# Output projection of a hybrid encoder layer: the attention half of the first 1024 columns by seven block products instead of eight

## The chip, the cores and the metric

One core of one Trainium2 chip runs the whole kernel. The metric is the device time of one execution in microseconds (us). The engines are named as the profile names them: PE (matrix products), PEld (weight loads of PE), ACT, DVE, POOL and SP (which only issues transfers). ACT and POOL issue transfers too.

## The reference, cut to what matters

One encoder layer is computed for 768 rows (a prompt of 512 and a sample of 256) of width 2048:

```python
h = rmsnorm(x, ln_mix_g); z = h @ w_in              # fourier group | q | k | v
of = fourier_mix(zf, w_fourier)                     # 768 x 1024
oa = window_attention(q, k, v, attn_sink)           # 768 x 1024
mixed = concatenate([rmsnorm(of, g_f), rmsnorm(oa, g_a)])
x = x + mixed @ w_out                               # 2048 x 2048; the second half of its rows meets oa
h = rmsnorm(x, ln_mlp_g); u = relu(h @ w_up); x = x + (u * u) @ w_down
return rmsnorm(x, ln_final_g)
```

The change is in the second half of `mixed @ w_out`: `oa` (768 x 1024) times rows 1024 to 2047 of `w_out`.

## The kernel before, in words

All arithmetic is float32 in effect: each operand of a product is split into a high part `h` (rounded) and a low part `l` (the rest), and a product is three matmuls, `h*wh + h*wl + l*wh`. ACT makes the high part by a copy (or a copy with a gain), DVE makes the low part by a subtraction.

Rows come in six tiles `m` of 128, columns of `w_out` in four groups `n` of 512, the 1024 channels of `oa` in eight blocks `k` of 128. In the stage of attention the Fourier half of `w_out` is multiplied in and put to memory as `y1_d[m][n]`; the attention blocks go to memory as `oa_d[m]` (transfers named `oad`) and come back as `oah`/`oal` (`load_oa`). The stage after it, called here the projection stage, does the attention half. For each `n` it takes three pairs of row tiles, `(mp, mp + 3)`; one pair is 48 matmuls of 512 columns into the two banks of `pm` (`proj_slot`). Then `x1_rows` adds: `sums` (DVE: `y1 + x`, which POOL has added up, plus `pm` times the row factor `r2`), `squares` (ACT), and `factors`: eight transposes on PE into `pt`, and `x1_factors` on DVE and ACT, which for `n < 2` makes the seven left factors `xf` of the next stage (`up_product`, which itself already works with seven products).

Weights come by `out_load(i)` (SP, 512 KB) and `out_split(i)`, where `i` numbers pieces of two `k` blocks by 512 columns; 16 to 19 are the attention half of `n = 0`, 20 to 23 of `n = 1`. `out_split` with a gain is, for each of the two `k` blocks, one ACT copy with the gain as scale and one DVE instruction.

The order of work is written by hand: `at(t, fn)` and `later(dt, fn)` put a step into a list by time, where one unit is six matmuls of 512 columns (two blocks `k` of one row tile, or one `k` of a pair), and `run_events(t)` is called between matmuls and records the steps that are due. Under `manual_schedule` PE, ACT, DVE, POOL and SP each run their instructions in the order in which they are recorded. So the list sets the order on every engine, and an instruction that waits holds up those recorded behind it on its engine. The DMA transfers of SP and ACT use eight semaphores (`DMAHW0` to `DMAHW7`) in turn, in the order in which they are recorded, and a transfer waits for the one that had its semaphore before it, which is the one eight places ahead.

## Time and profile before

| | |
|---|---|
| median of 3 runs | 2563.78 us (2563.24 to 2564.96) |
| the profiled execution, its own time | 2563.83 us |
| its span, first to last instruction | 2562.0 us |
| granted PE clock, mean | 0.999 |
| busy share of the span, PE / PEld / DVE / ACT / POOL | 100% / 91% / 71% / 44% / 11% |
| projection stage, first to last matmul start | 564.0 to 705.6 us |
| matmuls of 512 columns in it, besides 11 groups of 8 transposes | 576 |

Times in the profile are microseconds from the start of the span. Matmuls are pipelined: one of 512 columns is shown with some 389 ns, but the next starts after some 227 ns, so a short wait of PE hides in the overlap, and the count of matmuls in a stretch tells more than PE's busy share. `SPq` and `ACTq` are the issues of transfers.

### The profile page before, as it was taken

What the parts mean: (1) busy time and instruction counts of PE and PEld (TensorE: products, weight loads), DVE (VectorE), ACT (ScalarE), POOL (GpSimd) and SP (SyncE); (2) the same over time, 40 slices, a digit from 0 to 9 for tenths busy, and PEclk for the clock granted to TensorE, in tenths of its full rate; (3) what the DMA queues carried; (4) which work ended last, traced back from release to release, by engine and by line L of the source; (5) the groups of instructions that cost most, each with busy time, mean ns of one, the idle gap of its engine ahead of it and who ended that gap; (6) DMA issues with size and microseconds to landing.
All of it is one profiled execution on the core that took longest, in us unless ns stands there. A gap on an engine that the chain in (4) does not pass through costs nothing.

```text
span 2562.0 us, 34695 instructions
## 1 busy us (share of the span) xinstructions
PE 2552.0 (100%) x13415; PEld 2336.7 (91%) x13415; DVE 1810.6 (71%) x2144; ACT 1127.7 (44%) x1630; POOL 272.6 (11%) x387
## 2 busy tenths in 40 slices
PE   9999999999999999999999999999999999999998
PEld 9999998888899999999999999988888888888887
DVE  7877767678466556556777777667766756777687
ACT  7454557674233333334445454433333333333335
POOL 0023333223201010100000000200000000000000
PEclk9999999999999999999999999999999999999999
DMA  7686386465745444466666666775543662554364
GB/s 294 229 285 214 115 245 193 138 179 187 236 163 186 159 165 163 165 207 225 231 230 214 217 215 216 277 279 176 176 146 124 221 222 89 176 183 157 101 211 153
DMA packets 261029, 496.99 MB, mean 194 GB/s; under 512 B 21147, under 2 KB 145569, under 8 KB 260737
## 3 DMA queue, kind: packets, MB, share of 16 engines
q1 hardware_dynamic: 193600, 332.00, 40.7%
q10 hardware_dynamic: 51360, 101.43, 10.5%
q0 software_dynamic: 15904, 61.36, 7.1%
q8 instruction: 105, 1.72, 0.3%
q14 instruction: 60, 0.48, 0.1%
HBM read 373.19 MB, written 121.51 MB: 193 GB/s over the span
## 4 chain that ended last, share of the span: by engine, by line
PE 98%; DMA 1%; DVE 0%; ACT 0%; issue 0%; POOL 0%; SPq 0%; ACTq 0%; DVEq 0%; POOLq 0%
PE pu L1390 36%; PE pd L1825 35%; PE pm L1243 10%; PE p L287 7%; PE pz L1001 3%; PE pv L543 1%; PE o L1122 1%; PE s L1045 1%; PE t L1100 1%; PE pa L796 0%; PE ptx L138 0%; PE pe L815 0%; DMA ofd<-of 0%; DMA raw<-in_w_out 0%; DMA xr<-in_x_t 0%
## 5 line engine op out<-in xcount | busy, mean ns | idle before, releaser
L1390 PE MATMUL pu<-xf,wh 128*128 128x384 f32 x3072 | 780.2, 334 | 0.0
L1390 PEld LDWEIGHTS pu<-xf,wh 128*128 128x128 f32 x3072 | 554.1, 188 | 1.5 <-ACT o L1408 1.3
L1825 PE MATMUL pd<-wh,sh 128*128 128x512 f32 x1332 | 517.7, 389 | 0.0
L1825 PE MATMUL pd<-wl,sh 128*128 128x512 f32 x1332 | 517.7, 389 | 0.0
L1825 PE MATMUL pd<-wh,sl 128*128 128x512 f32 x1332 | 517.5, 389 | 0.0
L1390 PE MATMUL pu<-xf,wl 128*128 128x384 f32 x1536 | 513.1, 334 | 0.0
L1802 ACT ACTIVATE wh<-rd 128x1024 fp32r<-128x1024 f32 x200 | 202.4, 1054 | 522.3 <-PE pd L1825 424.4
L1812 DVE TENSOR_TENSOR wl<-rd,wh 128x1024 fp32r<-128x1024 f32 x200 | 236.1, 1221 | 226.2 <-ACT wh L1802 225.5
L1370 ACT ACTIVATE wh<-ur 128x1024 fp32r<-128x1024 f32 x160 | 170.1, 1063 | 382.6 <-PE pu L1390 226.7
L1825 PEld LDWEIGHTS pd<-wl,sh 128*128 128x128 f32 x1332 | 250.0, 188 | 51.9
L1825 PEld LDWEIGHTS pd<-wh,sh 128*128 128x128 f32 x1332 | 250.0, 188 | 51.9
L1825 PEld LDWEIGHTS pd<-wh,sl 128*128 128x128 f32 x1332 | 249.9, 188 | 51.8 <-DVE sl L1813 0.3
L1390 PEld LDWEIGHTS pu<-xf,wl 128*128 128x128 f32 x1536 | 288.3, 188 | 0.0
L1376 DVE TENSOR_TENSOR wl<-ur,wh 128x1024 fp32r<-128x1024 f32 x160 | 195.5, 1222 | 76.1 <-ACT wh L1370 76.1
L1411 DVE TENSOR_TENSOR o<-pu,o 128x768 f32<-128x768 f32 x160 | 152.9, 956 | 122.4 <-PE pu L1390 114.9
L287 PE MATMUL p<-xs,wh 128*128 128x384 f32 x672 | 170.6, 334 | 0.0
L1795 DVE TENSOR_TENSOR rd<-rd 128x1024 f32<-128x1024 f32 x112 | 131.7, 1217 | 0.0
L1390 PE MATMUL pu<-xs,wh 128*128 128x384 f32 x512 | 129.8, 334 | 0.0
L1370 ACT ACTIVATE wh<-sx 128x1024 fp32r<-128x1024 f32 x64 | 67.9, 1062 | 130.5 <-PE pu L1390 104.3
L287 PEld LDWEIGHTS p<-xs,wh 128*128 128x128 f32 x672 | 121.4, 188 | 0.1
L287 PE MATMUL p<-xs,wl 128*128 128x384 f32 x336 | 112.2, 334 | 0.0
L1813 DVE TENSOR_TENSOR sl<-sr,sh 128x768 fp32r<-128x768 f32 x111 | 105.6, 951 | 0.0
(309 smaller groups left out, 3774.9 us busy)
## 6 DMA issues: line engine op xcount, KB each, us to landing
rd<-in_w_down SPq DMA_DIRECT2D x176, 512.0 KB, 5.2
ur<-in_w_up SPq DMA_DIRECT2D x128, 512.0 KB, 3.8
sr<-sd SPq DMA_DIRECT2D x95, 384.0 KB, 5.4
pd<-o ACTq DMA_DIRECT2D x60, 384.0 KB, 2.3
o<-pd POOLq DMA_DIRECT2D x60, 384.0 KB, 6.2
sd<-sm ACTq DMA_DIRECT2D x60, 384.0 KB, 2.8
raw<-in_w_in SPq DMA_DIRECT2D x40, 512.0 KB, 5.1
raw<-in_w_out SPq DMA_DIRECT2D x32, 512.0 KB, 4.5
```

The source lines that it names most:

```text
L287: nc.tensor.matmul(ps7[own, g, r][:, :HALF], l[:, i, r * P : (r + 1) * P], x[:, o, 4 * e + i, :], start=(opens and e == 0 and i == 0 and q ...
L1001: nc.tensor.matmul(ps[c][s][:, :HALF], w[:, i, cs], whole[j // 2][s][o][:, 4 * (j % 2) + i, :], start=first and n == 0, stop=stop and n == 2,)
L1243: nc.tensor.matmul(ps, l(k), w[:, k % 2, :], start=(k == 0 and n == 0), stop=(k == 7 and n == 2))
L1370: nc.scalar.activation(wh[:], raw[:], AF.Copy)
L1376: nc.vector.tensor_tensor(out=wl[:], in0=raw[:], in1=f32(wh[:]), op=ALU.subtract)
L1390: nc.tensor.matmul(ps[:, t, :HALF], w[:, i, t * P : (t + 1) * P], xb[:, o, i, :], start=(s == first_of[bank] and i == 0 and n == 0), stop= ...
L1411: nc.vector.tensor_tensor(out=o, in0=src, in1=o, op=ALU.add)
L1795: add = lambda x, y, op: nc.vector.tensor_tensor(out=x[:], in0=x[:], in1=y[:], op=op)
L1802: nc.scalar.activation(wh[:], t[:], AF.Copy)
L1812: nc.vector.tensor_tensor(out=wl[:], in0=t[:], in1=f32(wh[:]), op=ALU.subtract)
L1813: nc.vector.tensor_tensor(out=sl[:], in0=sr[:], in1=f32(sh[:]), op=ALU.subtract)
L1825: nc.tensor.matmul(o, l[:, q, ts], w[:, ns], start=(j == j0 and (q, t) == (0, 0)), stop=(j == j1 and (q, t) == (1, 2)),)
```

## The change: what it does

For `n = 0` and `n = 1` the row tiles are taken as two blocks (tiles 0 to 2 and 3 to 5), the channels as two halves, and the 1024 columns as two halves, and the eight block products become seven, with sums of weight blocks (`ws1`, `ws2`, `s3`, `s4`) and of row blocks (`rows_sum`). The products run in the order of `steps`: a11, a12, s2, s1, s3, s4, a22. Each is 3 row tiles `p` by 4 `k` blocks by 3 matmuls. What a product gives is added by DVE into the rows that it belongs to (`add_rows`).

- Matmuls of 512 columns in this part: 7 x 36 = 252, before 288. `n = 2` and `n = 3` stay as they were, 288.
- Weights: pieces 16 to 19 (a11, a12) are split as before, but the gain is put in first, in place (`out_scale`, two ACT copies), and then comes one ACT copy and one DVE subtraction over the whole piece. The same is so for pieces 24 to 31. Blocks a21 and a22 (pieces 20 to 23) are loaded by `block_load` and scaled; a12 is loaded a second time. Ten further pieces are made by `block_high` and `block_low`, eight pieces' worth of sums by `block_sum`.
- Rows: for each `p`, four blocks of 128 x 512 are loaded a second time from `oa_d` (`rows_load`), four subtractions make the sums, and four splits the parts (`rows_parts`).
- Transposes and `x1_factors` of the first six pairs no longer stand between the products but beside `n = 2` and `n = 3`, at 42.8, 45.4, 48.0, 57.2, 64.3 and 72.3; the finished rows wait in `yq` and `op` tiles. The tile `xf` is opened only behind the products.

The diff, cut to its core:

```diff
     def out_split(i, more=True):
         half, n, j = out_seq[i]
-        k0 = half * 8 + 2 * j
-        out_w[half, n].append(wsplit(raws.pop(i), (lambda r: gcat[:, k0 + r : k0 + r + 1]) if half else None))
+        raw = raws.pop(i)
+        if half:
+            out_scale(i, raw)
+        out_w[half, n].append(wsplit(raw))
+        if 16 <= i < 18:
+            first_raw.append(raw)
...
+        def block_load(name):
+            for i, w in enumerate(ws[name]):
+                n, k0 = int(name[1]) - 1, 8 + 4 * (int(name[2]) - 1) + 2 * i
+                nc.sync.dma_start(w[:], w_out[:, k0 : k0 + 2, n * 512 : (n + 1) * 512])
...
+        def rows_sum(p, i):
+            b = rows[p]
+            x, y = ((1, 0), (2, 1), (2, 0), (3, 2))[i]
+            sub(b[i], b[x], b[y])
...
+        def rows_parts(f, p):
+            raw = rows[p][{3: 0, 4: 1, 5: 2, 6: 3}[f]]
+            nc.scalar.activation(th[f][p][:], raw, AF.Copy)
+            later(u_tl, lambda: sub(tl[f][p][:], raw, f32(th[f][p][:])))
...
+        block_load("a21")
+        rows_load(0)
+        block_load("a22")
+        for half in range(3):
+            turn_load(half, 0, None)
+        rows_load(1)
+        load_oa(5, lambda dt, fn: later(u_oa + dt, fn), spare)
+        rows_load(2)
+        block_scale("a21")
+        block_scale("a22")
+        rows_first(0)
+        at(0.2, lambda: rows_second(0))
+        at(0.3, lambda: row_factors(0, 5))
+        at(1.1, lambda: rows_first(1))
+        at(2.0, lambda: block_sum("s1", "a21", "a22", ALU.add))
+        at(4.0, lambda: block_sum("s2", "s1", "a11", ALU.subtract))
+        at(5.2, lambda: rows_second(1))
+        at(7.0, lambda: rows_first(2))
...
+        at(14.8, lambda: row_factors(5, 6))
+        for name, t in (("s2", 6.2), ("s1", 12.2), ("s3", 20), ("s4", 25), ("a22", 30.6)):
+            for i in range(2):
+                at(t + 1.1 * i, lambda name=name, i=i: block_high(name, i))
...
+        for q, (name, f, bank) in enumerate(steps):
+            for p in range(3):
...
+                for k in range(4):
+                    wh, wl = parts7[name][k // 2]
+                    for n, (o, w) in enumerate(((0, wh), (0, wl), (1, wh))):
+                        nc.tensor.matmul(
...
+        for half, t in enumerate((42.8, 45.4, 48.0, 57.2, 64.3, 72.3)):
+            at(t, lambda half=half: factors_of(half // 3, half % 3, yps.pop(half)))
```

The next three pieces show where the instructions stand. The first is the end of ACT's work for the attention stage: `raw` are the weight pieces 16 to 19, `os` and `xc` the last results that go to memory as `oad` and `y1`. Before:

```order
L72 ACTIVATE wh_6474<-raw_5853,gall_258 128x512 x2
L72 ACTIVATE wh_6488<-raw_5905,gall_258 128x512 x2
L1130 COPY os_6504<-o_6499 64x512
L72 ACTIVATE wh_6510<-raw_5931,gall_258 128x512 x2
L1275 ACTIVATE xc_6516<-pm_6447,r1_262 128x512
L1138 DMA oad5_97<-os_6504 64x4x128
L72 ACTIVATE wh_6519<-raw_5951,gall_258 128x512 x2
L1276 DMA y1_5_3_121<-xc_6516 128x512
```

The same place of the change:

```order
L171 ACTIVATE raw_5853<-raw_5853,gall_258 128x512 x2
L69 ACTIVATE wh_6476<-raw_5853 128x1024
L171 ACTIVATE raw_5905<-raw_5905,gall_258 128x512 x2
L69 ACTIVATE wh_6488<-raw_5905 128x1024
L1142 COPY os_6500<-o_6495 64x512
L171 ACTIVATE raw_5931<-raw_5931,gall_258 128x512 x2
L69 ACTIVATE wh_6508<-raw_5931 128x1024
L1287 ACTIVATE xc_6512<-pm_6447,r1_262 128x512
L1150 DMA oad5_97<-os_6500 64x4x128
L171 ACTIVATE raw_5951<-raw_5951,gall_258 128x512 x2
L69 ACTIVATE wh_6517<-raw_5951 128x1024
L1288 DMA y1_5_3_121<-xc_6512 128x512
```

Each weight piece has one more ACT instruction, of 1024 elements, and two whole pieces stand ahead of the copy `os`, whose result ACT's `oad5` transfer sends.

The second piece is SP's queue at the border of the two stages, with the semaphores for which each transfer waits. Before:

```order
L79 DMA raw_6480<-in_w_out 128x2x512 [waits DMAHW2_49,DVE_49]
L79 DMA raw_6494<-in_w_out 128x2x512 [waits DMAHW3_49,DVE_49]
L1547 DMA cx_6634<-y1_0_0_98 128x512 [waits DMAHW6_49,DMAHW5_49,DMAHW7_49,DMAHW1_49,DVE_49]
L1550 DMA xr_6636<-in_x_prompt 128x512 [waits PE_49]
L1547 DMA cx_6634<-y1_3_0_110 128x512 [waits DMAHW0_49]
```

The change, from the two transfers of block a22 to the third of the rows of `p = 1`:

```order
L1627 DMA wa22_6654<-in_w_out 128x2x512 [waits DMAHW2_49]
L1627 DMA wa22_6655<-in_w_out 128x2x512 [waits DMAHW3_49,Pool_49]
L1556 DMA yp_6662<-y1_0_0_98 128x512 [waits DMAHW4_49,DVE_49]
L1560 DMA xr_6678<-in_x_prompt 128x512 [waits DMAHW5_49]
L1556 DMA yp_6664<-y1_1_0_102 128x512 [waits DMAHW6_49,PE_49]
L1560 DMA xr_6682<-in_x_prompt 128x512 [waits DMAHW7_49]
L1556 DMA yp_6665<-y1_2_0_106 128x512 [waits DMAHW0_49]
L1560 DMA xr_6686<-in_x_prompt 128x512 [waits DMAHW1_49]
L1649 DMA b_6650<-oad1_93 128x4x128 [waits DMAHW2_49]
L1649 DMA b_6651<-oad4_96 128x4x128 [waits DMAHW3_49]
L1649 DMA b_6652<-oad4_96 128x4x128 [waits DMAHW4_49]
```

Eight places ahead of `wa22_6654` in the recorded order stands ACT's transfer `oad5<-os`, and eight ahead of `wa22_6655` ACT's `y1_5_3<-xc`, the last two of the first piece (SP's six between them, `wa21` twice and `b` four times, are recorded behind these two). `b_6651` has the semaphore of `wa22_6655`.

The third piece is DVE. Behind the low parts of the four weight pieces and the four row sums of `p = 0` stands this, up to the first weight piece of product s2 (`wl_6808`), which PE reads from its 74th matmul of the stage on:

```order
L1608 TENSOR_TENSOR b_6652<-b_6652,b_6650 128x512
L1635 TENSOR_TENSOR ws1_6630<-wa21_6648,wa22_6654 128x1024
L1635 TENSOR_TENSOR ws1_6631<-wa21_6649,wa22_6655 128x1024
L1581 SCALAR_TENSOR_TENSOR yp_6662<-pm_6713,r2_263,yp_6662 128x512
L1635 TENSOR_TENSOR ws2_6628<-ws1_6630,raw_5853 128x1024
L1635 TENSOR_TENSOR ws2_6629<-ws1_6631,raw_5905 128x1024
L1581 SCALAR_TENSOR_TENSOR yp_6664<-pm_6735,r2_263,yp_6664 128x512
L1608 TENSOR_TENSOR lb_6641<-b_6646,hb_6638 128x512
L1608 TENSOR_TENSOR b_6653<-b_6653,b_6652 128x512
L1608 TENSOR_TENSOR lb_6642<-b_6652,hb_6639 128x512
```

and behind these, in this order, one more `add_rows`, three row sums of `p = 2`, and `wl_6808`; ahead of the first row stand the sums `b_6650` and `b_6651`. In the kernel before DVE had here, behind the low parts of the weights:

```order
L1575 SCALAR_TENSOR_TENSOR cx_6634<-pm_6653,r2_263,cx_6634 128x512 x2
L70 TENSOR_TENSOR oal5_6642<-cx_6634,oah5_6641 128x512 x2
L98 TENSOR_SCALAR r2_263<-pr_6744 128x1 x2
L1306 TENSOR_TENSOR cx_6777<-ptx_6751,gall_258 128x512 x2
L1313 TENSOR_TENSOR cx_6777<-cx_6777 128x512
L1313 TENSOR_TENSOR cx_6777<-cx_6777 128x256 x2
```

The sums of rows and weights thus stand in one queue with the adding up of the products, and the factors of `xf` have left this place.

More of the change, by code (lines that the diff above doesn't have):

```diff
@@ new lines, in turn_loads, with row_factors @@
+        def turn_loads(half):
+            yp = op.tile([P, 2, 512], F32, tag=f"of{'lh'[half % 2]}5", name="yp")
+            yps[half] = [yp[:, s, :] for s in range(2)]
+            for s in range(2):
+                turn_load(half, s, max(8 * half - 6 + u_xr - clock[0], 2.3))
+        def row_factors(m0, m1):
+            pr = pq.tile([P, 2, 512], F32, tag="pt", name="pr", bufs=1)
+            for m in range(m0, m1):
+                nc.tensor.matmul(pr[:, 0, m : m + 1], oa[m][2][:], ones[:, 0:1], start=True, stop=True)
+            rsqrt_of(r2[:, m0:m1], pr[:, 0, m0:m1], NH * HD, m1 - m0)
@@ new lines, in hybrid_encoder @@
+        ws = {"a11": first_raw, "s1": ws1, "s2": ws2, "a21": wa21, "a22": duo("wa22")}
+        rows.append(four(2))
+        spare = [sp.tile([P, 4, P], F32, tag=f"ob{i}", name="ob")[:] for i in range(2)]
+        ws["s3"], ws["s4"], ws["a12"] = ws["a21"], ws["s2"], ws["s1"]
+        def block_load(name):
+            for i, w in enumerate(ws[name]):
+                n, k0 = int(name[1]) - 1, 8 + 4 * (int(name[2]) - 1) + 2 * i
+                nc.sync.dma_start(w[:], w_out[:, k0 : k0 + 2, n * 512 : (n + 1) * 512])
```

211 lines of the change are left out of this document (143 added, 68 removed).

## The prediction

> **What bounds the kernel now.** I read the page first, its busy shares and the chain that ended last.
>
> ```profile
> PE 2552.0 (100%) x13415; PEld 2336.7 (91%) x13415; DVE 1810.6 (71%) x2144; ACT 1127.7 (44%) x1630; POOL 272.6 (11%) x387
> ...
> PE 98%; DMA 1%; DVE 0%; ACT 0%; issue 0%; POOL 0%; SPq 0%; ACTq 0%; DVEq 0%; POOLq 0%
> ```
>
> The chain is PE for 98% of the span. Next the waits of PE, all of them:
>
> ```profile
> PE pw L566 <- DVE ssx L133: 1.0, 1, 1.0
> PE pv L543 <- ACT xs L72: 0.6, 1, 0.6
> PE pm L1245 <- DVE ofl L1227: 0.3, 1, 0.3
> PE pm L1243 <- ACT ofh L1226: 0.2, 1, 0.2
> ```
>
> None lies in the projection stage. A matmul taken away is therefore worth its full interval, and a wait put in costs its full length. The interval is read from the chain in order of time:
>
> ```profile
> 563.48 6.14 PE pm L1243 x27
> 569.62 0.34 PE pr L1564 x4
> ...
> 582.28 10.94 PE pm L1243 x48
> ```
>
> 48 matmuls of 512 columns take 10.94 us, 0.228 each. By the view of the tile `pm` the stage starts at 564.0:
>
> ```profile
> L1243 PE MATMUL pm<-wh,oah x192: 389/389/486, 564.0 to 705.1; 128*128 128x512 f32 x192
> ```
>
> DVE's mean of 71% says little about this stage, so I read it in stretches:
>
> ```profile
> 588.00:612.00 24.00, 24.00 (x118) 20.14 (x117) 21.40 (x32) 12.58 (x21) 4.00 (x4) 1.00 0.59 194
> ...
> 636.00:660.00 24.00, 24.00 (x115) 20.06 (x115) 14.70 (x20) 6.14 (x12) 5.58 (x4) 1.00 0.65 201
> 660.00:684.00 24.00, 24.00 (x115) 20.05 (x115) 12.22 (x17) 8.08 (x17) 5.16 (x4) 1.00 0.76 249
> 684.00:705.80 21.80, 21.80 (x106) 18.20 (x106) 6.44 (x8) 4.84 (x10) 5.87 (x5) 1.00 0.68 220
> ```
>
> The fourth busy time is DVE's: 21.4 of 24 us in one stretch of the first half, 33 of 70 in the last three. The change gives DVE more work early in the stage, where it must be done before a product can start.
>
> **What is removed.** 288 - 252 = 36 matmuls: 36 x 0.228 = 8.2 us. The eighty-eight transposes and six single columns for the row factors stay in number and only move, so they cost nothing more on PE unless they wait.
>
> **The first product that needs new operands.** Products a11 and a12 use the old rows and pieces 16 to 19; s2 follows behind 72 matmuls, at 564.0 + 72 x 0.228 + 0.34 (the row factors) = 580.7. Its second matmul needs `wl_6808`. I follow the three queues to it. ACT first, from its timeline at the end of the attention stage:
>
> ```profile
> 558.86 0.69 ACT L1104 ACTIVATE th<-t,r 128x512 fp32r<-128x512 f32 x1
> 558.88 0.58 ACTq L1276 DMA_DIRECT2D y<-xc  x1
> 559.51 2.57 ACT L72 ACTIVATE wh<-raw,gall 128x512 fp32r<-128x512 f32 x4
> 563.51 0.58 ACT L1130 COPY os<-o 64x512 f32<-64x512 f32 x1 [1.44 <-PE o L1122]
> ...
> 564.85 0.61 ACTq L1138 DMA_DIRECT2D oad<-os  x1
> ...
> 566.08 0.33 ACTq L1276 DMA_DIRECT2D y<-xc  x1
> ```
>
> ```profile
> L1802 ACT ACTIVATE wh<-rd 128x1024 fp32r<-128x1024 f32 x200 | 202.4, 1054 | 522.3 <-PE pd L1825 424.4
> ...
> L1812 DVE TENSOR_TENSOR wl<-rd,wh 128x1024 fp32r<-128x1024 f32 x200 | 236.1, 1221 | 226.2 <-ACT wh L1802 225.5
> ```
>
> A scale of 512 takes 0.64 (2.57 for four), a copy of 1024 elements 1.05, so a weight piece takes ACT 2.33 where it took 1.28. Two pieces from 559.5 end at 564.2, ACT's `os` at 564.75. DVE makes `wl_6489` from 564.2 to 565.4 and the sum for `oad5` by 566.0: the transfer is issued 1.2 us later than now. The fourth piece's scales are done at 568.9, and only then, its `y1_5_3`, 2.8 later than now. The fourth piece ends at 570.0 and DVE's low part of it at 571.2; PE needs these pieces from 572 on, so here nothing waits.
>
> SP now. What a transfer takes, by the DMA view of the stage (the last figure), and what the engines carried when busy:
>
> ```profile
> raw<-in_w_out SPq DMA_DIRECT2D x12, 512.0 KB, 4.2
> ...
> oar<-oad SPq DMA_DIRECT2D x4, 256.0 KB, 2.9
> y<-xc ACTq DMA_DIRECT2D x4, 256.0 KB, 3.3
> ...
> oad<-os ACTq DMA_DIRECT2D x4, 128.0 KB, 3.4
> ```
>
> ```profile
> 555.00:560.00 5.00, 5.00 (x28) 4.13 (x27) 3.20 (x5) 3.63 (x6) 0.35 (x1) 1.00 0.10 19
> ...
> 575.00:580.00 5.00, 5.00 (x24) 4.14 (x23) 1.93 (x3) 1.75 (x3) 3.26 (x4) 1.00 0.94 331
> ```
>
> ```profile
> 569.26 0.34 SPq L1547 DMA_DIRECT2D cx<-y  x1
> 569.65 0.42 SPq L1550 DMA_DIRECT2D xr<-in_x_prompt  x1
> ```
>
> Such a wait is real now: SP's first `y` load goes out at 569.26, 3.2 us behind ACT's `y1` transfer of 566.08, one of those it waits for. In the change `wa21` and the rows of `p = 0` go out before 563 into almost idle engines (19 GB/s), which costs nothing. `wa22_6654` waits for `oad5`: 566.0 + 3.4 = 569.4. `wa22_6655` waits for `y1_5_3`: 568.9 + 3.3 = 572.2, and everything behind it on SP waits with it: six loads for `yp` and `xr`, at 0.42 an issue, then the rows of `p = 1`. Lower bound for the third of these: `b_6651` waits for the landing of `wa22_6655`, 572.2 + 4.2 = 576.4, and lands 2.9 later, 579.3. Upper bound: half a megabyte, six quarters and three quarters, 2.88 million bytes, share 331 GB/s: 8.7 us, and 2.1 of latency (2.9 less 0.8 for 256 KB): 572.2 + 10.8 = 583.0. I take 582, near the upper end, since all ten are in the queue at once.
>
> DVE last. From `b_6650` to `wl_6808` it runs seventeen instructions: nine of 512 elements, three with PSUM, five of 1024. Their prices, from the timeline and the page:
>
> ```profile
> 546.29 1.31 DVE L70 TENSOR_TENSOR oal<-oar,oah 128x512 fp32r<-128x512 f32 x2
> ...
> 578.07 1.41 DVE L1575 SCALAR_TENSOR_TENSOR cx<-pm,r,cx 128x512 f32<-128x512 f32 x2 [7.85 <-POOL r L101]
> 579.40 3.21 DVE L70 TENSOR_TENSOR oal<-cx,oah 128x512 fp32r<-128x512 f32 x2
> ...
> 590.29 1.07 DVE L1174 TENSOR_REDUCE sr<-cx 128x128 f32<-128x512 f32 x1
> ```
>
> ```profile
> 579.09 2.97 POOL L1555 TENSOR_TENSOR yp<-yp,xr 128x512 f32<-128x512 f32 x2 [0.52 <-DMA xr<-in_x_prompt]
> ```
>
> 9 x 0.655 + 3 x 0.70 + 5 x 1.18 (1.22 shown, less the overlap that the smaller ones have) = 13.9 us. Two subtractions that take 1.31 alone took 3.21 beside two of POOL's additions, 0.95 lost to each; between none and four of POOL's additions (`yp` of the second row block) fall into the 14 us. I take two, 1.9. So `wl_6808` is there at 582 + 13.9 + 1.9 = 597.8, and **PE waits 17.1 us**; between 579.3 + 13.9 - 580.7 = 12.5 and 583.0 + 13.9 + 3.8 - 580.7 = 20.0.
>
> **Behind it.** `wl_6826` comes 2 x 0.655 + 1.18 = 2.5 after, and PE has five matmuls, 1.1, until then: 1.4 of wait. The row factor of tile 5, between the second and third row tile of s2, needs `sr_6695`, six instructions and a reduction after `wl_6826` (4 x 0.655 + 2 x 0.70 + 1.07 = 5.1); PE has 17 matmuls, 3.9: 1.2 of wait. By then the later parts have been made up behind PE's wait, and DVE runs at about PE's pace; the next products wait between 0 and some 2 us.
>
> The six sets of factors that move beside `n = 2` and `n = 3` were hidden under PE in the first half. One set is this on DVE:
>
> ```profile
> 594.53 1.29 DVE L1306 TENSOR_TENSOR cx<-ptx,gall 128x512 f32<-128x512 f32 x2 [0.39 <-PE ptx L138]
> 595.85 1.61 DVE L1313 TENSOR_TENSOR cx<-cx 128x512 f32<-128x512 f32 x3
> ...
> 598.70 2.09 DVE L1321 TENSOR_TENSOR xf<-cx,xf 128x512 fp32r<-128x512 f32 x2
> ```
>
> 5.0 us; six are 30, on top of the 33 of 70 us: 63 of 70, so it still fits on average. But the first three stand 2.6 units apart, 2.6 x 6 x 0.228 = 3.6 us, with one tile `pt`: the second and the third set wait some 1.4 each for DVE, and other pieces in the queue add. With the products behind s2 I take 5 us for all later waits, between 0 (what the trace of before shows) and 9 (a set's excess, 1.4, for each of the six).
>
> **The sum.** -8.2 + 17.1 + 1.4 + 1.2 + 5 = +16.5 us. The profiled execution took 2563.83 us, within 0.05 of the median; 2563.8 + 16.5 = 2580.3, so 2580. Lower end: -8.2 + 12.5 + 1.4 + 1.2 + 0 = +6.9, 2571. Upper: -8.2 + 20.0 + 1.4 + 1.2 + 9 = +23.4, 2587.
>
> **A rule against the change.** In every stretch shown the granted clock of PE is 1.00, and PE never waits longer than 1.0 us, so no row tells what follows a wait of 17. The Trainium skill, "TensorE: Matmul & The Clock Gate", section on the HAM clock gate, says that the array falls to half its clock after an idle window of about 3.4 us and returns after about 3.4 us of work. By that page the sum would be some 1.7 to 3.4 us higher, an estimate; no run here shows it.
>
> **The rivals.**
> 1. The loads are in time, and only DVE's own work stands in the way. For it: SP is free from 551 and the engines are idle from 555 to 560; if block a22 and the rows of `p = 1` did not hang on ACT's last transfers, DVE would run straight on from 571.2: 4 x 0.655 + 13.9 later is 587.7, a wait of 7.0, and -8.2 + 7.0 + 1.4 + 1.2 = +1.4: 2565, no change. Against it: the order of SP's waits.
> 2. The other side: the operands of s2 are ready at 580.7, all later waits stay under 0.3 as now, and the saving is kept: 2563.8 - 8.2 = 2555.6. It is decided by one point, whether DVE can start the seventeen instructions by 580.7 - 13.9 = 566.8. For it: in the kernel before PE had no wait here. Against it: the four low parts ahead of them end at 571.2.
> 3. PE comes back slowly from its wait. If the granted clock were halved for the next 15 matmuls, each would take 0.228 more, 3.4 in all; with a second such wait, in the two steps of `wh_6795` and `wl_6808`, up to 6.8: 2584 to 2587. For it speaks no row; against it, 1.00 everywhere. This is the rule above, as a case of its own.
> 4. DVE never catches up: each of the four products behind s2 waits the 2 us given above as the most, and the moved sets cost their 9: -8.2 + 20.0 + 2.6 + 8 + 9 = +31.4, 2595. For it: 21.4 of 24 us busy where less was asked of DVE; against it: it works on while PE waits.
>
> **How the numbers follow.** About 0.2%, 5.1 us, is what a measurement of this kernel tells from no change. I give the main case 0.62, the slow return 0.12, DVE behind throughout 0.12, the loads in time 0.09, the saving kept 0.05. The first three are slower: 0.86; the fourth is no change, the fifth faster. The main case holds 2571 to 2587; the range takes in half of the fourth rival and the edge of the first, 2568 to 2591, which leaves out some 2 in 10.
>
> **What would show it.** In the profile after: a wait of PE of 12 to 20 us near 581, in one or two pieces, on `wl` or `wh` of s2, the longest of the run; SP's `wa22` issues at 569 and 572; DVE without a gap from about 582 to 598; 252 and 288 matmuls of `pm`; short waits of `ptx` on DVE in the second half. I am wrong if the rows of `p = 1` land before 576, or if DVE's seventeen instructions take under 10 us; the clock's row decides the third rival.

## The result and the profile after

The changed kernel takes 2600.25 us (median of four runs, 2598.05 to 2602.68), the kernel before beside it 2563.82: a ratio of 1.0142, 95% interval 1.0124 to 1.0159, 36.4 us slower. The profiled execution has a span of 2599.6 us against 2562.0. The prediction was 2580, 2568 to 2591: the sign was right, the size was wrong, and the time lies above the range.

The page, busy times and the chain that ended last:

```profile
PE 2556.5 (98%) x13379; PEld 2336.7 (90%) x13379; DVE 1849.0 (71%) x2171; ACT 1158.1 (45%) x1668; POOL 274.3 (11%) x383
...
PE 94%; DVE 3%; ACT 1%; issue 1%; DMA 1%; SPq 0%; POOL 0%; ACTq 0%; DVEq 0%; POOLq 0%
```

The 36 matmuls are gone (13415 less 13379), yet PE is busy 4.5 us longer. The waits of PE between 560 and 760 us (total, times, longest), none of which was there before:

```profile
PE pm L1740 <- DVE wl L1608: 11.9, 3, 9.6
PE pm L1740 <- ACT wh L1639: 10.6, 1, 10.6
PE ptx L138 <- DVE yp L1581: 8.4, 4, 4.8
PE ptx L138 <- DVE cx L1318: 2.2, 2, 1.8
PE pm L1255 <- ACT pm L1584: 0.8, 1, 0.8
```

33.9 us in all. The two longest, 10.6 and 9.6, are the two pieces of the first wait, 20.2 us; the rest, 13.7, comes later. Where they stand, by PE's timeline (in brackets the idle time ahead and what ended it):

```profile
591.80 0.80 PE L1740 MATMUL pm<-wh,hb 128*128 128x512 f32 x1 [10.56 <-ACT wh L1639]
602.20 0.80 PE L1740 MATMUL pm<-wl,hb 128*128 128x512 f32 x1 [9.60 <-DVE wl L1608]
...
623.56 0.50 PE L1740 MATMUL pm<-wl,hb 128*128 128x512 f32 x1 [1.81 <-DVE wl L1608]
625.79 0.80 PE L1740 MATMUL pm<-wl,hb 128*128 128x512 f32 x1 [0.52 <-DVE wl L1608]
...
679.86 1.97 PE L138 MATMUL ptx<-ident,yp 128*128 128x128 f32 x8 [2.62 <-DVE yp L1581]
...
710.06 1.68 PE L138 MATMUL ptx<-ident,yp 128*128 128x128 f32 x8 [4.80 <-DVE yp L1581]
```

And by stretches, with the granted clock (third figure from the end) and PE's and DVE's busy times (second and fourth figure):

```profile
585.00:605.00 20.00, 3.59 (x8) 2.47 (x9) 19.83 (x21) 4.82 (x7) 7.51 (x5) 0.50 0.67 227
605.00:610.00 5.00, 5.00 (x18) 3.96 (x16) 4.37 (x8) 3.84 (x9) 0.00 (x0) 0.70 0.17 68
...
625.00:630.00 5.00, 4.48 (x11) 3.35 (x11) 5.00 (x5) 1.20 (x2) 1.85 (x1) 0.50 0.08 29
630.00:640.00 10.00, 10.00 (x42) 8.18 (x41) 9.37 (x12) 5.55 (x9) 0.00 (x0) 0.91 0.01 5
...
680.00:690.00 10.00, 10.00 (x46) 8.58 (x47) 4.16 (x7) 1.86 (x5) 1.72 (x2) 0.85 0.66 211
...
710.00:720.00 10.00, 9.94 (x45) 8.35 (x46) 5.25 (x7) 3.59 (x8) 0.29 (x1) 0.83 0.62 202
```

PE comes back from four of its waits at half clock: what is missing to 1.00 in these rows makes 2.9 us behind 602 (half of the 2.8 us up to 605, 0.30 of 5), 3.1 behind 625.8 (half of 4.5, 0.09 of 10), 1.5 and 1.7, together 9.2. The account of the span: -8.2 + 33.9 + 9.2 = +34.9 of the measured +37.6. Most of the rest is the way in which waits are counted: idle time begins where a matmul is shown to end, 0.16 us after the next would have started (0.389 less 0.227), and 11 waits make that 1.8 us, an estimate.

DVE through the first wait, then POOL and SP at that place:

```profile
584.36 2.18 DVE L1608 TENSOR_TENSOR b<-b 128x512 f32<-128x512 f32 x3 [10.52 <-DMA b<-oad]
...
595.20 1.75 DVE L1608 TENSOR_TENSOR lb<-b,hb 128x512 fp32r<-128x512 f32 x1
596.87 0.74 DVE L1581 SCALAR_TENSOR_TENSOR yp<-pm,r,yp 128x512 f32<-128x512 f32 x1
597.53 3.48 DVE L1608 TENSOR_TENSOR b<-b 128x512 f32<-128x512 f32 x3
600.94 1.21 DVE L1608 TENSOR_TENSOR wl<-ws,wh 128x1024 fp32r<-128x1024 f32 x1
```

```profile
593.34 3.06 POOL L1561 TENSOR_TENSOR yp<-yp,xr 128x512 f32<-128x512 f32 x2 [0.29 <-DMA xr<-in_x_sample]
```

```profile
568.24 5.11 SPq L1627 DMA_DIRECT2D wa<-in_w_out  x2
```

DVE has the rows of `p = 1` at 584.4 and then runs without a gap to 602.1, 17.8 us; five of POOL's additions fall into that time (from 591.79 to 600.46). The subtraction at 595.20 took 1.75 beside POOL's additions; the row addition at 596.87, which reads one operand from PSUM, took its usual 0.74, though POOL went on adding (596.55 to 598.07). The Trainium skill, "SBUF — State Buffer", section "Who interferes with whom", says that a DVE instruction with two SBUF inputs shares its second read interface with POOL, and one with a single SBUF input does not; the two rows agree.

### The profile page after: what moved, and what is told of

Its sections match the earlier page's. It is cut to its first block, busy times and chain, and to the rows that moved or that the text cites. A ratio compares the mean times of both kernels' runs of the same rounds, so it can differ in the third digit from the quotient of the medians.

```text
span 2599.6 us, 34718 instructions
## 1 busy us (share of the span) xinstructions
PE 2556.5 (98%) x13379; PEld 2336.7 (90%) x13379; DVE 1849.0 (71%) x2171; ACT 1158.1 (45%) x1668; POOL 274.3 (11%) x383
## 4 chain that ended last, share of the span: by engine, by line
PE 94%; DVE 3%; ACT 1%; issue 1%; DMA 1%; SPq 0%; POOL 0%; ACTq 0%; DVEq 0%; POOLq 0%
PE pu L1402 36%; PE pd L1976 35%; PE p L299 7%; PE pm L1255 6%; PE pz L1013 4%; PE pv L555 1%; PE o L1134 1%; PE s L1057 1%; PE t L1112 1%; PE pm L1740 1%; DVE cx L1325 1%; PE pe L827 0%; PE pa L808 0%; ACT raw L171 0%; PE ptx L138 0%
```

## The experiments

Four theories. **1**: transfers that go out late, and the order of the queues, keep operands from PE. **2**: DVE takes too long for its work beside the products, whatever its order, be it by the amount or because POOL works beside it. **3**: the half clock behind each wait is a cost of its own. **4**: the moved factor sets stand ahead of the row sums in DVE's queue. The runs, each beside the kernel before (2563.7 to 2564.4 us); the last column adds up PE's waits between 560 and 745 us in the profiled execution, which for the changed kernel took 2601.38 us and for all_three 2574.06, its shortest:

| run | us | ratio to before | waits, us |
|---|---|---|---|
| changed kernel | 2600.25 | 1.0142 (1.0124 to 1.0159) | 33.9 |
| other_queue | 2596.17 | 1.0125 (1.0110 to 1.0140) | 28.9 |
| other_queue_order | 2595.86 | 1.0124 (1.0107 to 1.0141) | 25.1 |
| no_x_additions (two times) | 2593.59 | 1.0115 (1.0094 to 1.0135) | 28.6 |
| late_sums | 2591.78 | 1.0107 (1.0091 to 1.0124) | 30.5 |
| dma_additions | 2584.82 | 1.0081 (1.0066 to 1.0096) | 19.7 |
| dma_and_late | 2582.60 | 1.0069 (1.0054 to 1.0084) | 20.4 |
| all_three | 2577.03 | 1.0049 (1.0034 to 1.0064) | 13.3 |
| filled_waits | 2602.83 | 1.0152 (1.0137 to 1.0167) | 14.5 |
| filled_shorter | 2600.99 | 1.0142 (1.0127 to 1.0157) | 12.9 |
| before_dma_additions | 2564.98 | 1.0002 (0.9992 to 1.0011) | 0.9 |
| forced_waits (one time) | 2638.31 | | |

### Loads on another queue

```diff
-        block_load("a22")
-        rows_load(1); load_oa(5, ...); rows_load(2)
+        block_load("a22", nc.gpsimd)
+        rows_load(1, nc.gpsimd); rows_load(2, nc.gpsimd); load_oa(5, ..., nc.gpsimd)
```

> The transfers of a22, of the rows of p=1 and p=2 and of oad5 are issued by POOL, whose transfers are counted on semaphores of their own, instead of SP, where they wait for ACT's last stores; nothing else is changed. In the changed kernel these issues stood at 568 to 580 us, DVE idled 10.5 us for the rows of p=1 until 584.4, and PE waited 10.6 + 9.6 us around its first product s2. Theory 1 (the wait comes from the late issue): a22 and the rows that need no late heads come some 5 us earlier, DVE's idle stretch falls from 10.5 us to under 4, the first wait from about 21 us to 10 to 15, the time falls by 6 to 11 us. Theory 2 (DVE's own queue is the bound): DVE's idle stretch shrinks too, but PE's first wait stays above 18 us since the 17.8 us of DVE work behind it set it. A rival for both: POOL issues no sooner, because its queue holds the row additions or the writes of oad5 land late, and nothing moves (within 3 us).

Measured: 4.1 us less, short of the 6 to 11 that theory 1 asked for. The rows were there at once; the next thing was late. DVE's timeline:

```profile
576.29 2.14 DVE L1608 TENSOR_TENSOR b<-b 128x512 f32<-128x512 f32 x3
586.58 0.75 DVE L1581 SCALAR_TENSOR_TENSOR yp<-pm,r,yp 128x512 f32<-128x512 f32 x1 [5.88 <-POOL r L101]
```

DVE's 10.5 us of idle time before the rows of `p = 1` are gone, and 5.9 are back in another place: the first row addition needs the row factor `r2`, and POOL takes its power (L101) behind its own first additions. PE's first wait is 15.4 us in place of 20.2.

### The same, and another order on DVE

```diff
-        at(1.1, rows_first(1)); at(2.0, s1 sum); at(4.0, s2 sum); at(7.0, rows_first(2))
+        at(0.4, s1 sum); at(0.5, s2 sum); at(1.9, rows_first(1)); at(3.0, rows_first(2))
-        s2 parts at 6.2 and 7.3, rows_parts(5, p) at 4.4, 5.1, 8.4
+        s2 parts at 0.8 and 1.0, rows_parts(5, p) at 0.7, 2.0, 3.1
```

> As the run before, and besides DVE and ACT take the sums s1 and s2 and the high and low parts of s2 ahead of the row differences of p=1 and p=2 and ahead of the first row additions (the same instructions in another order). Until the first matmul of s2 DVE then has about 3 row differences, the two block sums (4.7 us), one low part of the rows (0.6 us) and two of the block (2.4 us), some 10 us in place of 17.8. If load time and DVE's queue together make the first wait (theories 1 and 2), it falls to 0 to 6 us in all, and with it most of the half-clock stretch behind it: 15 to 22 us faster than the changed kernel, about 2578 to 2585 us. If the wait were set by something else (the late row product, the additions of POOL), it stays above 10 us.

Measured: 4.4 us less than the changed kernel, no more than the run before and far from the expected 15 to 22. The low part is no longer what PE waits for; the row addition is, which must read the bank before s2 adds to it (DVE's timeline, then PE's):

```profile
584.37 4.14 DVE L1608 TENSOR_TENSOR b<-b 128x512 f32<-128x512 f32 x3
...
589.56 0.74 DVE L1581 SCALAR_TENSOR_TENSOR yp<-pm,r,yp 128x512 f32<-128x512 f32 x1
```

```profile
590.45 0.76 PE L1740 MATMUL pm<-wh,hb 128*128 128x512 f32 x1 [5.97 <-DVE yp L1581]
598.95 0.48 PE L1740 MATMUL pm<-wh,hb 128*128 128x512 f32 x1 [3.04 <-DVE yp L1581]
```

The power of the row factor was ready here at 588.85 and DVE came to the row addition without a gap, so it was DVE's queue that made it late, with three subtractions that took 4.14 beside POOL's additions and 2.18 alone (584.36 in the changed kernel). Theory 1 holds for the first cause and not for the size: behind the late loads stands a second late thing.

### POOL's additions left out, and made by transfers

```diff
-            add = lambda: nc.gpsimd.tensor_tensor(out=yp[s], in0=yp[s], in1=xr, op=ALU.add)
+            add = lambda: None                                             # no_x_additions, halves 0 to 5
+            add = lambda: nc.gpsimd.dma_start(yp[s], x_rows(m)[...], accum_op=ALU.add)   # dma_additions, all 24, no load of xr
```

> Leaves out POOL's additions of the input rows to the first twelve tiles of the projection (so their residual is missing from the output); their transfers stay. In the changed kernel DVE's differences took 1.74 us instead of 0.66 beside these additions, and PE's first wait ended 17.8 us of DVE work after the rows of p=1 landed. If POOL beside DVE is part of the loss, that stretch falls to about 14 us, the first wait from 21 to 16 to 18 us, the wait at 622 to 626 us (beside two additions of 1.9 us each) shrinks by 2 us, and the time falls by 3 to 6 us. If DVE would only wait elsewhere, it falls by under 1.5 us.

> The input rows are added to the first-half outputs by transfers that add where they land, in place of a load and POOL's addition, for all 24 tiles; the output is the same. Leaving out 12 of POOL's additions made the time 6.7 us shorter (9.7 us by the spans). If it was POOL beside DVE that cost this, the additions by transfers bring the same: 2589 to 2595 us, DVE's differences at 0.66 to 0.72 us each in the window of the first wait and not 1.74. If it was the load's transfer or something in the removed waits, or if POOL's making of the transfers' descriptors slows DVE as much, the time stays within 2 us of the changed kernel's 2600.

Measured: 6.7 and 15.4 us less. DVE in the window of the first wait, first with POOL's additions left out, then with additions by transfers:

```profile
585.21 2.17 DVE L1608 TENSOR_TENSOR b<-b 128x512 f32<-128x512 f32 x3 [10.48 <-DMA b<-oad]
...
597.66 1.22 DVE L1608 TENSOR_TENSOR wl<-ws,wh 128x1024 fp32r<-128x1024 f32 x1
```

```profile
583.26 2.26 DVE L1604 TENSOR_TENSOR b<-b 128x512 f32<-128x512 f32 x3 [7.36 <-DMA b<-oad]
...
592.49 0.68 DVE L1604 TENSOR_TENSOR lb<-b,hb 128x512 fp32r<-128x512 f32 x1
...
595.80 1.22 DVE L1604 TENSOR_TENSOR wl<-ws,wh 128x1024 fp32r<-128x1024 f32 x1
```

From the rows of `p = 1` to the low part, the same instructions take 13.7 us without POOL's additions (585.2 to 598.9) and 13.8 with additions by transfers (583.2 to 597.0); 13.9 was the prediction's figure without POOL. They took 17.8 in the changed kernel: POOL beside DVE cost 4.0 in this window alone. The first of the two runs still has the `xr` loads, so it was the additions that slowed DVE and not these loads. The second edit also takes the `xr` loads out of SP's queue, and the waits at 623 to 626 and three of the four for row sums at the later transposes go (0.3 and 3.3 us are left of 2.3 and 8.4). It gained far more than I expected, and it does two things at once (POOL's adds and 24 loads). For the first wait the two runs show the split: 20.2 us became 16.0 without POOL's additions but with the loads, and 13.0 without either. For the later waits the split isn't shown.

> The kernel before, with its 24 additions of the input rows made by transfers in place of loads and POOL additions. Where PE never waits in this stage, nothing should come of it: within 1.5 us of the kernel before. If it is faster by more than 3 us, the additions cost the kernel before too and the gain of the same edit in the changed kernel is not about its DVE queue.

In the kernel before, the same edit is worth nothing (1.0002): there PE doesn't wait for DVE. The additions cost time only where PE waits for DVE.

### The moved sets' sums later

```diff
-        for half, t in enumerate((42.8, 45.4, 48.0, 57.2, 64.3, 72.3)):
+        for half, (t, late) in enumerate(((42.8, 0), (45.9, 0), (49.0, 3.0), (57.2, 1.0), (64.3, 1.6), (72.3, 1.6))):
```

> In the six moved factor sets the block sums and the parts behind the gain product wait 1 to 3 units (1.4 to 4.1 us) longer on DVE, so that the row sums of the later halves stand ahead of them in DVE's queue; the second and third sets begin 0.5 and 1 unit later. Nothing else is changed. In the changed kernel PE waited 8.4 us for those row sums at its later transposes (2.6, 0.6, 4.8, 0.3 us), and the clock was 0.85 and 0.83 in the two stretches of 10 us behind the longer two, some 3 us more. Theory 4 (the moved sets stand in front of the row sums): these waits fall under 2 us and the clock stays at 1.00, 6 to 11 us faster: 2589 to 2594 us. Theory 2 (DVE has too much work whatever its order): other waits come in their place and the time falls by under 3 us.

Measured: 8.5 us less. PE's waits at the transposes:

```profile
PE ptx L138 <- DVE cx L1318: 3.7, 4, 2.5
...
PE ptx L138 <- DVE yp L1588: 1.5, 1, 1.5
```

8.4 us of waiting for row sums became 1.5, 1.5 more went to the gain products, and the clock column between 640 and 720 us is 1.00 throughout. The part of the stage that the edit touches, `n = 2` and `n = 3`, takes 83.1 us (650.7 to 733.8) where it took 91.3 (651.6 to 742.9): 8.2 less, of which 5.1 are waits (11.4 became 6.3) and 3.2 the half clock behind them. Theory 4 holds.

### Is the half clock a cost of its own?

```diff
+                if p == 0 and q in (2, 4):      # ahead of s2 and s3
+                    for c in range({2: 94, 4: 28}[q]):      # filled_shorter: 94 and 14
+                        nc.tensor.matmul(warm[:, c % 2, :], ...)      # nobody reads it
```

> PE is given work in its two longest waits of the weight products: 94 matmuls of 512 columns whose result nobody reads (94 x 0.227 = 21.3 us) ahead of the first matmul of s2, and 28 (6.4 us) ahead of the first of s3; DVE, ACT and the transfers keep their order, so nothing comes sooner. If the half clock after the waits costs time of its own (theory 3), the matmuls behind stand 0.227 us apart from the start instead of 0.427: the stretch of s2 from 602.2 ends 2.9 us sooner (but DVE, which is busy throughout until 626, takes that back at s3), and the stretch from 625.8 ends 2.9 us sooner for good: 2 to 5 us faster in all, 2595 to 2598 us. If the half clock is no loss of its own (PE would have to wait for DVE anyway), the time stays within 1 us or rises by it.

> As the filled waits, but with 14 filler matmuls (3.2 us) in place of 28 ahead of s3: in that run PE's fillers there ended 2.7 us after DVE had what s3 needs, so that they stood on the path. The forced waits showed 1.5 to 2.8 us lost at half clock behind each wait of 3.8 to 18.3 us. If the half clock in the changed kernel costs time where DVE isn't the bound (theory 3), the stretch behind 625.8 runs at full clock and the time is 2 to 4 us below the changed kernel's 2600.25, at 2596 to 2598 us; if DVE's queue takes all of it back, 2599 to 2601 us.

Measured: 2602.83 and 2600.99 us. In the second, by stretches:

```profile
585.00:605.00 20.00, 19.34 (x86) 15.66 (x85) 19.83 (x21) 4.84 (x7) 8.18 (x6) 1.00 0.68 227
...
625.00:630.00 5.00, 5.00 (x24) 4.14 (x23) 5.00 (x5) 2.80 (x4) 2.72 (x2) 1.00 0.12 44
...
640.00:680.00 40.00, 34.27 (x159) 27.77 (x158) 27.34 (x32) 20.28 (x34) 6.14 (x4) 0.96 0.51 165
680.00:690.00 10.00, 10.00 (x42) 8.12 (x41) 4.20 (x7) 0.63 (x1) 3.01 (x2) 0.82 0.54 158
690.00:710.00 20.00, 14.85 (x74) 12.01 (x73) 13.36 (x18) 12.88 (x19) 2.57 (x2) 0.94 0.56 184
710.00:720.00 10.00, 10.00 (x42) 8.20 (x42) 5.03 (x6) 2.59 (x6) 1.61 (x2) 0.79 0.80 249
```

The clock is 1.00 where it was 0.50, as meant. PE is 2.5 us ahead at the first transposes (652.9 against 655.4), 1.0 at the end of the stage, and the time is the same. Behind 602 the full clock brings nothing: PE reaches the eighth matmul of s3, the first that needs the second low part, at 626.2 where it did at 625.8, held by DVE, which has this part ready at 624.8, and then by the fillers themselves for 1.4 us more. Behind 625.8 it brings the 2.5. These go later: the waits between 640 and 745 us are nearly the same (10.9 for 11.4), but what is missing to 1.00 between 640 and 720 is 6.2 us here and 3.2 in the changed kernel, for a reason that these runs don't show. So the unchanged time doesn't show that the half clock is free. What the half clock itself is, the forced waits show:

```diff
+    def hold_pe(ps, k):                    # kernel before, units 3, 9, 15, 21, 27, 33 of the last stage
+        for n in (0, k):                   # k = 1, 2, 4, 8, 16, 32
+            for _ in range(n): nc.gpsimd.tensor_tensor(out=zero[:], in0=ones[:], in1=ones[:], op=ALU.subtract)
+            nc.tensor.matmul(ps[:, :P], zero[:], zero[:], start=False, stop=False)
```

> The kernel before, with six waits forced on PE in the last stage, 51 us apart, where it otherwise runs without a gap: PE multiplies a zero tile into an open sum, POOL rewrites the zeros 1, 2, 4, 8, 16 or 32 times, and PE multiplies them again. It adds 12 matmuls and some POOL work and measures what a wait costs beyond itself. Theory 3 (PE comes back at half clock after a wait): behind the waits of over some 2 us the matmuls of 512 columns stand 0.427 us apart for 3 to 6 us and then 0.227, a loss of 1.5 to 3 us each; behind those of about 1 us nothing. If the half clock came from something else in the changed kernel's stage (its transfers, its DVE load), the matmuls stand 0.227 apart right behind every wait.

Measured: 74.1 us more, of which 56.8 are the six waits. Two of them, PE's timeline:

```profile
1788.10 0.33 PE L1888 MATMUL pd<-zero 128*128 128x128 f32 x1 [4.39 <-POOL zero L1883]
...
1789.41 0.63 PE L1825 MATMUL pd<-wh,sh 128*128 128x512 f32 x1
1789.83 0.63 PE L1825 MATMUL pd<-wl,sh 128*128 128x512 f32 x1
...
1791.96 0.39 PE L1825 MATMUL pd<-wh,sh 128*128 128x512 f32 x1
1792.19 0.39 PE L1825 MATMUL pd<-wl,sh 128*128 128x512 f32 x1
...
1980.70 0.47 PE L1888 MATMUL pd<-zero 128*128 128x128 f32 x1 [18.34 <-POOL zero L1883]
```

Matmuls start 0.42 to 0.43 us apart behind the wait and 0.23 later. Behind waits of 10.4, 3.8, 4.4, 8.0, 11.8 and 18.3 us this lasts 6.0, 3.6, 3.7, 6.0, 3.4 and 5.6 us, a loss of 1.6 to 2.9 each, with no order by the length of the wait. All six waits were at least 3.8 us, so those of about 1 us, which I had meant to include, weren't tried. Theory 3 holds for the mechanism. As a term of the sum the half clock has no one price: behind 602, where PE next waits for DVE, it was hidden; behind 625.8 it cost 2.5 of its 3.1 us; and at the transposes, by late_sums, 3.2 us of it went together with the waits.

### Together, and what is left

The two edits on additions and late sums; then these with the other queue, the order on DVE, the power ahead of the additions and the last row product 2 units later:

```diff
-            turn_load(half, 0, None)
+            turn_load(half, 0, 1.0)                  # POOL: the power first
-        at(14.8, lambda: row_factors(5, 6))
+        at(16.8, lambda: row_factors(5, 6))
```

> The changed kernel with the additions by transfers and the late sums, without the other queue and order. Alone they gained 15.4 and 8.5 us; the waits that they removed lie partly at the same places (the later transposes waited 8.4 us for row sums, with the additions by transfers still 3.3). Expected 2576 to 2582 us: if it is 2576 or less, the two are independent and the loads' queue and DVE's order bring nothing more (all three: 2577.0); if it is 2581 or more, queue and order are worth 4 us or more.

> Together: the loads on POOL's queue with DVE's other order, the additions by transfers, the late sums, and besides the row factor's power on POOL ahead of the first additions (in the run with loads and order PE waited 9.0 us for row additions that waited for it) and the row factor of the last tile 2 units later (3.2 us waited). All matmuls of the changed kernel stay. If the loss is made up of these waits and of the half clock behind them, they go together: 2600 less some 4 for loads and order, 9 for the row factor, 7 for the additions, 8 for the late sums and 3 for the row product, about 2570 us (2560 to 2580), so about what the kernel before takes; at best the 36 matmuls are kept as a gain, 2556. If DVE's amount of work is the bound (theory 2), PE waits for it in other places and the time stays above 2582 us.

Measured: 2582.60 and 2577.03. The gains of 15.4 and 8.5 don't add (17.7 together), since both empty the same waits at the transposes; queue, order and power are worth 5.6 more. Of the loss 23.2 us are back, and 12.8 over the kernel before remain. Seven more runs went to that rest. The edits of the first two and of the two that take work from DVE:

```diff
+        rows_load(0, nc.gpsimd); block_load("a22", nc.gpsimd); rows_load(1, nc.gpsimd)
+        turn_load(half, 0, None) for the first three       # tuned: here; all_more: behind load_oa(5)
+        rows_load(2, nc.gpsimd); load_oa(5, ..., nc.gpsimd)
-        at(3.0, lambda: rows_first(2))
+        at(4.4, lambda: rows_first(2))
+        at(16.0, ...), at(16.2, ...), at(16.4, ...)         # tuned: rows_second(0 to 2), before at 0.2, 5.2, 9
+        at(20.6, lambda: row_factors(5, 6))                 # tuned; tuned_order and order_and_row_lows: 23.6
+        load_oa(5, lambda dt, fn: later(10 + dt, fn), ...)  # tuned, before u_oa = 3; tuned_order and order_and_row_lows: 7
+        at(22.0 if (q, p) == (2, 2) else t, add_rows ...)   # tuned; tuned_order and order_and_row_lows: 25.1
...
-            later(u_tl, lambda: sub(tl[f][p][:], raw, f32(th[f][p][:])))
+            later(u_tl, lambda: nc.scalar.activation(tl[f][p][:], raw, AF.Copy, scale=0.0))    # row_lows_off_dve
-            sub(wl[:], ws[name][i][:], f32(wh[:]))
+            nc.scalar.activation(wl[:], ws[name][i][:], AF.Copy, scale=0.0)                    # all_lows_off_dve, besides
```

> As all three together, with what still waited there mended: all rows' loads on POOL's queue, so that SP issues the outputs' loads 10 us sooner; the first additions ahead of the power; DVE's row additions of the first product ahead of the next row differences; the last tile's row product 2 units later (2.2 us waited); s1's parts 0.8 units earlier (2.0 us waited). PE waited 13 us in all in the run before. If these are still queue and order (theory 1), half of it goes: 2567 to 2573 us. If DVE's amount of work in the weight products is the bound (theory 2: it was busy 50 of 53 us there, for 41 us of PE's products), the waits move and the time stays within 3 us of 2577. Level with the kernel before (2564) only if nearly all of it goes.

> All three together, and in DVE's queue of the weight products what is needed only later stands later: the fourth row differences (needed by the last product), the parts, squares and row product of the last heads; the row differences of p=2 stand behind the first row additions; the first three additions by transfers are issued between the rows of p=1 and p=2, the rows of p=0 by POOL too, so that the outputs' loads leave SP sooner. No instruction is added or left out. If order is what is left of the loss (theory 1), the waits of the weight products (9.1 us with all three together) go: 2564 to 2569 us, level with the kernel before. If the amount of DVE's work is (theory 2), DVE stays gapless to some 620 us and PE waits at another product: 2574 us or more.

> As the tuned run, and the gain products of the six moved factor sets are made by ACT (four activations of 256 columns for two DVE products of 512), which takes some 7.7 us of work from DVE in the second part of the stage. There PE still waited 3.4 us at transposes with all three together (for the gain product's release of the one PSUM tile 2.5, for row sums 0.9). Theory 2: those waits go, 2 to 4 us below the tuned run. Theory 1, or a full ACT queue (ACT holds the high parts of the weights there): within 1.5 us of the tuned run, or slower.

> The tuned run (2576.1 us) with the twelve low parts of the row differences set to zero by ACT (0.6 us each there) in place of DVE's differences (0.66 us each): leaves the second-order term of these four factors out of the product, 7.9 us of DVE work less, every other instruction as it was. In the tuned run DVE stood gapless from 570.7 to 624.5 us. Theory 2 (DVE's amount of work beside the weight products is what is left): most of it comes back, 2568 to 2572 us. Theory 1 (the order, or a load): within 2 us of 2576.

> The run before, and besides the ten low parts of the weight block sums set to zero by ACT too (1.06 us each there in place of 1.21 us on DVE): 20 us of DVE work less in all, the second-order terms of five products left out. Theory 2: DVE then has some 33 us of work beside 41 us of PE's products, is no bound there, and the time comes within a few us of the kernel before or under it: 2558 to 2566 us, since the change's 36 matmuls (8.2 us) are then kept as a gain less the 4 to 5 us that the later transposes wait. If it stays at 2568 or more, something other than DVE's work holds PE in this stage.

> The tuned run (2576.1 us) with order changed alone: the row product of the last heads 3 units later (PE waited 3.6 us for it there, and the 5 us behind ran at clock 0.50) and what it feeds behind it, their parts and squares 3 units earlier, the moved sets' sums behind the gain product of the set that follows (PE waited 2.0 us for that), s1's parts 0.3 units earlier. All of DVE's work is back that the two runs before took out, where 7.9 and 20 us less of it gave 0.2 and 2.3 us. If the order is what is left (theory 1), the row product's wait and its half clock go, some 6 us, and 2 us at the transposes: 2566 to 2570 us. If the time stays at 2574 or more, the small waits move on to other places, as they did from all three to the tuned run.

> The last order (without the later moved sums, which cost a wait of 3.5 us at 688) together with the row differences' low parts set to zero by ACT: 7.9 us of DVE work less and the row product out of PE's way; leaves the second-order term of four factors out. Each alone gave nothing (575.9 and 576.7 after 576.1, plus 2000 us). If the two causes cover each other (while DVE is behind, moving the row product only uncovers the next low part; while the row product holds PE, less DVE work is not seen), both together give what neither gave: 2566 to 2571 us. If the time stays at 2574 or more, the rest is neither.

| run | edit, in short | us | waits, us |
|---|---|---|---|
| all_more | `rows_load(0)` by POOL too; `rows_first(2)` 3.0 to 4.4, and six more steps moved | 2582.42 | 17.5 |
| tuned | first additions between `rows_load(1)` and `(2)`; `rows_second` at 16; `row_factors(5, 6)` at 20.6 | 2576.12 | 12.5 |
| tuned_gain_on_act | tuned, `cx` by `nc.scalar.activation(..., scale=gm)` | 2576.97 | 12.0 |
| row_lows_off_dve | tuned, `tl` by `nc.scalar.activation(..., scale=0.0)`: zeros, their term is left out | 2575.91 | 11.8 |
| all_lows_off_dve | that, and the ten `wl` | 2573.85 | 11.7 |
| tuned_order | tuned, `row_factors(5, 6)` at 23.6, sums of the last sets 3.0 later | 2576.73 | 15.3 |
| order_and_row_lows | both kinds, the sums of the last sets as in tuned | 2578.76 | 17.1 |

all_more was a mistake of mine: the first additions by transfers stood behind the rows of `p = 2` on POOL's queue, and DVE idled 5.0 us for them. In the others the waits change place. `tuned`, then `all_lows_off_dve`, then `tuned_order`, waits of PE:

```profile
PE pr L1580 <- DVE sr L1186: 3.6, 1, 3.6
PE ptx L138 <- DVE cx L1318: 2.9, 3, 2.0
PE pm L1743 <- DVE yp L1584: 2.7, 1, 2.7
```

```profile
PE pr L1580 <- DVE sr L1186: 3.6, 1, 3.6
...
PE pm L1743 <- ACT wl L1647: 1.8, 2, 1.4
PE pm L1743 <- ACT wh L1642: 1.6, 1, 1.6
```

```profile
PE pm L1743 <- DVE wl L1611: 5.0, 2, 2.5
PE ptx L138 <- DVE yp L1584: 3.5, 1, 3.5
PE pm L1743 <- DVE yp L1584: 3.4, 2, 2.7
```

Of theory 2 the part on POOL is shown above; the part on the amount is not borne out: 7.9 and 20 us of DVE's work less gave 0.2 and 2.3 us, the second not clear of the spread (tuned 2574.30 to 2577.41 us, this run 2573.19 to 2576.16). These edits give the same work to ACT, though, and PE's waits for ACT in the second view come with it, so a kernel with less DVE work and no more for ACT wasn't tried. Order alone gave nothing either: with the row product moved, its 3.6 us came back as waits for `wl` and `yp`; and with both kinds of edit, DVE idled 4.5 us for the power of the last row factor, which POOL took late. So far as these runs go, each longer wait ended on a chain through two or three queues (ACT, DVE, POOL, a transfer), and moving one step uncovered the next. What an order that covers them all would give, and whether there is one, stays open. None of the 18 kernels is faster than the one before.

## Why the prediction was wrong

- **The saving.** 36 matmuls less, as said; on PE they are worth 8.2 us.
- **The first wait.** The place, the two pieces and the cause are as predicted: SP's issues of `wa22` (one at about 568, the other by 573.4, for 569.4 and 572.2), PE there at 580.9 (580.7). The size was 20.2 us, for 17.1 and an upper end of 20.0. Two terms failed. DVE had the rows of `p = 1` at 584.4, not 582, and above the bound of 583.0. And POOL beside DVE cost 4.0 us, not 1.9: five of POOL's additions fell into the window, where I took two and four as the most (3.8). I had also taken the loads for the one thing in the way; the other_queue run shows that the power of the row factor stood right behind.
- **The waits behind it** for `wl_6826` and the row factor (1.4 and 1.2) didn't come: PE ran at half clock there and met them late. With the clock at 1.00, in filled_shorter, they came, 0.7 and 1.3 us.
- **The later waits** are the first of the two steps that failed most: 13.7 us (33.9 less 20.2) for 5, and above the bound of 9. The pace of the first three sets was right in kind (0.4 and 1.8 us for `cx`, where I had 1.4 each). But I weighed only the sets against each other. What they stood in front of, the row sums of the later halves in the same queue, cost 8.4 us of waiting, and late_sums shows it. "63 of 70 us, so it fits on average" was the wrong argument, since an in-order queue isn't an average.
- **The clock** is the second: the sum put it at nothing, and it is 9.2 us of the account, slightly more than the later waits are off (8.7). The third rival had it, with a chance of 0.12 and one or two places; it happened four times. 1.00 in the kernel before was no evidence against it, for PE never waited there longer than 1.0 us. The rule named with it, the Trainium skill's "TensorE: Matmul & The Clock Gate", section on the HAM clock gate, agrees in kind: half clock after an idle window of about 3.4 us. The trace adds that 1.8 and 0.5 us within 4 us were enough at 625.8, and 2.6 at 679.9. Not every one of these stretches costs its full length: with two of the waits filled, the one behind 602 gave nothing back and the one behind 625.8 gave 2.5 us, which more half clock at later waits took again.
- **The fourth rival**, DVE behind throughout, came nearest in time (2595) by a mechanism that is half right: DVE was behind, but by POOL and by order. That its amount of work alone makes the rest was not borne out by the runs on it.
- **The sum, term by term**: +3.1 in the first wait, -2.6 in the two behind it, +8.7 in the later ones and +9.2 for the clock take +16.5 to the account's +34.9. **The range** let the unknowns be independent; two terms lay above their bounds, and the clock had none.

## What to carry to other kernels

Where an in-order queue has slack on average, look at what each inserted block of work stands in front of: the cost is that row's lateness, and it is paid at the engine that waits for it. When you mean to remove a wait on the path, list the second and third latest operand first; here loads, a power on POOL and DVE's order each hid the next. An engine that slows another one costs nothing while nobody waits for the slowed engine (1.0002 in the kernel before), and it became the largest single item here (15 of 36 us, with its loads) where PE did.

## What the chip showed beyond expectation

- Behind the forced waits, matmuls of 512 columns run 0.42 to 0.43 us apart for 3.4 to 6.0 us, whether the wait was 3.8 or 18.3 us; once, behind 3.8 us, the first three still ran at 0.22 to 0.24. Length doesn't decide it for short waits either: 2.6 us at 679.9 in the changed kernel brought the half clock, 2.5 us at 709.5 in late_sums did not.
- DVE's subtraction of 512 columns from SBUF takes 0.68 us alone and up to 1.75 beside POOL's additions, an addition with one operand in PSUM 0.74 in both cases.
- Additions made by the transfers themselves cost POOL some 0.9 us of issue each and left DVE at 0.68.
